# Hybrid encoder step on one core: norm scale of the second layer's first block moved into the first layer's last head, first pair's preparation moved to round 5

## The chip, the cores and the metric

The kernel runs on one NeuronCore of one Trainium2 chip. The metric is the device time of one execution in microseconds (us), and the median of several runs is what counts. The trace names the engines PE (matrix products; PEld are its weight loads), DVE (vector), ACT (scalar), POOL (GpSimd) and SP, whose queue issues all DMAs of this kernel.

## The reference, cut to what matters

One step of a two-layer encoder over 2048 prompt tokens and 8 running streams of 16 tokens, all in float32. Layer 0 is a gated DeltaNet (below: layer A, 8 heads), layer 1 is RWKV-7 (layer B, 16 heads, worked on as 8 pairs).

```python
def rms_norm(x, w):
    return x * rsqrt(mean(x * x, axis=-1) + 1e-6) * w
def trunk(x, ...):
    for i in range(2):
        h = rms_norm(x, norm_w[i])
        y = mixer_a(h, ...) if i % 2 == 0 else mixer_b(h, ...)
        x = x + y
    return rms_norm(x, final_norm_w), ...
def mixer_b(h, x_prev, s0, mu, w_in, ...):
    xx = concat(x_prev, h[:, :-1]) - h
    xs = h + xx * mu[g]                      # g = 0..5
    r, k, v, z = (xs[g] @ w_in[:, g] for g in range(4))
    w_log = -softplus(-(w0 + tanh(xs[4] @ w_w1) @ w_w2)) - 0.5
    a = sigmoid(a0 + (xs[5] @ a_w1) @ a_w2)
    ...                                      # recurrence, group norm, gate with silu(z), @ w_out
```

What the change touches is the factor rsqrt(mean(x * x)) of layer B's norm for the first 256 tokens (the "scale").

## The kernel before, in words

Activations lie with channels on the 128 partitions (8 slices k of the 1024 channels) and tokens along the row. Every large product is made of three float32r matmuls (high part by high, by low, and low weight by high: `gemm`, and L451 to L453, L1059 to L1061), so each weight and each activation is split by an ACT cast and a DVE or POOL subtraction. On first use a weight is loaded raw, split and written back as a pair; later blocks load the pair.

**Layer A** takes five token blocks of 3 or 4 chunks of 128 tokens. `a_steps` counts i over 40 heads of all blocks and three more steps. In step i, `weave` runs side by side: the recurrence of head i-2 (`a_rec`), the Gram matrices and inverse of head i-1 (`a_gram`), the output product of head i-3 (`a_out`), at block ends the next block's norm, and the slots of a stream of large input products. `weave` interleaves generators by the share of the step that each is given; every `yield` ends one slot. At i = 40 the stream of layer A is used up. `swap` (in `layers`) closes the right-hand pool of tiles, opens that of layer B in its place and returns layer B's stream; steps 40, 41 and 42 take 33, 34 and 34 slots of it (AHEAD = 101).

**Layer B** takes six blocks: 128 prompt and 128 sample tokens (NT = 256), then five of 384 tokens. `b_stream` first runs `b_hidden` of block 0: `norm_scale` (8 squares on ACT, 6 additions on DVE and POOL, column sums on PE at L204, rsqrt, spread over the partitions on PE at L216), 18 slots with the 9 idle ones that `wait` = 8 asks for, then the normalised rows H (L991), 4 slots. Then come 136 slots per block of two-product units in the order g = 1 (K), 0 (R), 4 with 5 (the two low-rank products, "LoRA"), 2 (V), 3 (gate z): 8 slots per pair of products, and 6 matmuls in a slot. Their inputs, the lerps x + xx mu, are made by `b_lerp` in up to 8 buffers; most are made in bursts at fixed slots, 16 of them during the LoRA pair. `b_keep` copies a finished product into one of two "kvo" buffers and stores it in DRAM. The LoRA results pass through the same two buffers and are split into the tiles LT, of which there is one copy.

`b_steps` runs 54 steps i of 12 rounds each. In step i: `b_prep` of pair i, `b_subst` of pair i-1, `b_inverse` of i-2, `b_scan` of i-3, `b_gate` of i-4, in odd steps `b_out`, now and then `b_final`, and 17 slots of the stream (PACE; 8 from i = 40 on). `rounds` gives each part the round numbers of its slots; what is left of a part is run in round 12. `b_prep` begins with two products that read LT and the pair's weight w2 (L1120), which `b_load` fetches one step earlier (L1096, split at L1098 and L1099).

PE executes in the order of the program text (MANUAL). For the other engines and the DMA queue a list scheduler sets the order at compile time, by due times that `_due` works out from the next use, and it frees a tile's memory when all its readers are done.

Of the kernel before, what the change touches and what calls it, by code (L numbers as in the profile page):

```python
# [9 lines left out]
F32 = mybir.dt.float32  # L10
# [6 lines left out]
P = 128  # L17
# [54 lines left out]
class _K:  # L72
# [191 lines left out]
    def layers(self):  # L264

        tc, nc = self.tc, self.nc
        ab, bb, off = [], [], 0
        for npc, nsc in A_BLOCKS:
            n = npc + nsc
            ab.append(dict(off=off, npc=npc, nsc=nsc, n=n, NT=n * P, NP=npc * P))  # L270
            off += n * P
        off = 0
        for ncp, nsc in B_BLOCKS:
            nq = ncp + 2 * nsc
            bb.append(dict(off=off, ncp=ncp, nsc=nsc, nq=nq, NP=ncp * 64, NT=nq * 64))
            off += nq * 64
        with ExitStack() as st, ExitStack() as main, ExitStack() as side, tc.manual_schedule(engines=MANUAL):
            self.psum = st.enter_context(tc.tile_pool(name="psum", bufs=1, space=bass.MemoryType.PSUM))
            self.wpool = st.enter_context(tc.tile_pool(name="wpool", bufs=1))
            self.mp = main.enter_context(tc.tile_pool(name="amain", bufs=1))  # L280
            self.sp = side.enter_context(tc.tile_pool(name="aside", bufs=1, side="right"))
            self.a_setup()

            def swap():
                side.close()
                self.sp = side.enter_context(tc.tile_pool(name="bside", bufs=1, side="right", reuse_waits="tile"))
                self.b_setup_side()
                return self.b_stream(bb)
            stream = self.a_steps(ab, swap)
            main.close()  # L290
            self.mp = main.enter_context(tc.tile_pool(name="bmain", bufs=1, reuse_waits="tile"))
            self.b_setup()
            self.b_steps(bb, stream)
# [24 lines left out]
            S.append(s)  # L318
        self.cw, self.hist, self.nw, self.abc, self.nega, self.S = cw, hist, nw, abc, nega, S

    def a_steps(self, blocks, swap):

        nc, n = self.nc, len(blocks) * HA

        def at(i):
            return (blocks[i // HA], i % HA) if 0 <= i < n else None
        st = self.a_stream(blocks, self.a_first(blocks[0]))

        def take(i):
            for end in st:  # L330
                if end and i + 1 < n:
                    return
                yield
        for i in range(n + 3):
            if i == n:
                self.put_conv()
                st = swap()
            parts = []
            if at(i - 2):
                b = at(i - 2)[0]  # L340
                parts.append((self.a_rec(*at(i - 2)), 11 + 3 * b["npc"] + 7 * b["nsc"], 0.3 if i == 2 else 0.0, 1.0))
            if at(i - 1):
                parts.append((self.a_gram(*at(i - 1)), 17, 0.0, 0.95))
            if at(i - 3):
                parts.append((self.a_out(*at(i - 3)), 13, 0.1, 1.0))
            if i % HA == HA - 1 and at(i + 1):
                parts.append((self.a_norm(blocks[i // HA + 1]), 9, 0.0, 0.8))
            if i < n:
                parts.append((take(i), 24 if i % HA else 31, 0.0, 1.0))
            else:  # L350
                m = AHEAD * (i + 1 - n) // 3 - AHEAD * (i - n) // 3
                parts.append((islice(st, m), m, 0.0, 1.0))
            self.weave(parts)
        for h in range(HA):
            nc.sync.dma_start(self.io["o_pd"][h], self.S[h])
        return st
# [571 lines left out]
    def b_steps(self, blocks, st):  # L928

        npair = len(blocks) * KT  # L930
        def at(i):
            return (blocks[i // KT], i % KT) if 0 <= i < npair else None
        self.b_load(*at(0))
        for i in range(npair + 6):
            parts = []
            if at(i):
                parts.append((self.b_prep(*at(i)), range(1, 13)))
            if at(i - 2):
                parts.append((self.b_inverse(*at(i - 2)), (1, 2, 3, 4, 5, 6, 7, 8, 10)))
            if at(i - 4):  # L940
                parts.append((self.b_gate(*at(i - 4)), (1, 2, 3, 6)))
            if at(i - 1):
                parts.append((self.b_subst(*at(i - 1)), range(1, 9)))
            if at(i - 3):
                b = at(i - 3)[0]
                parts.append((self.b_scan(*at(i - 3)), 2 * b["ncp"] + 6 * b["nsc"], 0.0, 1.0))
            j = i - 5
            if at(j) and j % 2 == 0:
                out = self.b_out(blocks[j // KT], (j % KT, j % KT + 1))
                if j < npair - 2:  # L950
                    parts.append((out, 8, 0.5, 1.0))
                else:
                    parts.append((chain(out, self.b_final(blocks[j // KT])), 21, 0.5, 1.0))
            if at(j) and j % KT == KT - 1 and j < npair - 1:
                parts.append((self.b_final(blocks[j // KT]), 13, 0.0, 1.0))
            m = PACE if i < npair - KT else LAST_PACE
            parts.append((islice(st, m), m, 0.0, 1.0))
            self.rounds(ROUNDS, parts)
            if at(i + 1):
                self.b_load(*at(i + 1))  # L960
        for p in range(KT):
            self.nc.sync.dma_start(self.io["o_pw"][p], self.R[p])

    def b_hidden(self, b):

        nc, io = self.nc, self.io
        off, NP, NT, nsc = b["off"], b["NP"], b["NT"], b["nsc"]

        def xs(k):
            x = self.sp.tile([P, NT], F32, name=self.nm("xn"), tag="xn", bufs=2)  # L970
            nc.sync.dma_start(x, self.x1d[:, k, off:off + NT])
            return x
        rb = yield from self.norm_scale(xs, NT, 8 if off == 0 else 0)
        HT = self.sp.tile([P, KT * (1 + NP + (NS * (TS + 1) if nsc else 0))], F32, name=self.nm("H"), tag="H", bufs=1)
        H = HT[:, 0:KT * (1 + NP)].rearrange("p (k t) -> p k t", k=KT)
        nc.gpsimd.tensor_copy(H[:, :, 0:1], self.hc)
        if nsc:
            Hs = HT[:, KT * (1 + NP):].rearrange("p (k s t) -> p k s t", k=KT, t=TS + 1)
            sh0 = self.sp.tile([P, KT, NS], F32, name=self.nm("sh"), tag="sh", bufs=1)
            nc.sync.dma_start(sh0, io["shift_s"])  # L980
            nc.gpsimd.tensor_copy(Hs[:, :, :, 0:1], sh0.unsqueeze(3))

        def cur(k):
            o = [(slice(0, NP), H[:, k, 1:1 + NP], H[:, k, 0:NP], lambda a: a)]
            if nsc:
                o.append((slice(NP, NT), Hs[:, k, :, 1:], Hs[:, k, :, 0:TS], lambda a: a.rearrange("p (s t) -> p s t", t=TS)))
            return o
        for k in range(KT):
            x = xs(k)
            for sl, h, _, v in cur(k):  # L990
                nc.vector.scalar_tensor_tensor(h, v(x[:, sl]), self.nrm[:, 1, k:k + 1], v(rb[:, sl]), op0=MUL, op1=MUL)  # L991
            if k % 2:
                yield
        nc.gpsimd.tensor_copy(self.hc, H[:, :, NP:NP + 1])
        if off + NT == NTOK:
            nc.sync.dma_start(io["o_ph"], self.hc.rearrange("p k o -> p (k o)"))
        if nsc:
            sh = self.sp.tile([P, KT, NS], F32, name=self.nm("sh"), tag="sh", bufs=1)
            nc.gpsimd.tensor_copy(sh.unsqueeze(3), Hs[:, :, :, TS:TS + 1])
            nc.sync.dma_start(io["o_sh"], sh)  # L1000
        b["cur"] = cur
# [667 lines left out]
```

## Time and profile before

| what | us |
|---|---|
| median of 3 runs | 4665.8 |
| lowest and highest | 4654.6 and 4667.97 |
| the profiled execution, own time | 4661.34 |
| its span, first to last instruction | 4659.5 |

The rows below are of the one profiled execution; times in them are us from the start of its span unless marked ns. PEclk is the clock granted to PE as a share of full speed. Number in square brackets: idle time of the engine before the instruction, and who ended it. Layer A ends and layer B begins at about half of the span.

### The profile page before, as it was taken

How to read it: one execution, taken by the hardware profiler on the slowest of the kernel's cores; microseconds unless marked ns; L12 is line 12 of the kernel's file. 1: busy time of each engine (PE TensorE's matmuls, PEld its weight loads, DVE VectorE, ACT ScalarE, POOL GpSimd, SP SyncE). 2: the span in 40 equal slices, each digit the busy share in tenths (PEclk: the TensorE clock that was granted, in tenths of full speed). 3: DMA queues.
4: the chain of work that ended last, by engine and by line, in shares of the span. 5: the costliest groups of instructions: out<-in, count | busy, mean ns of one | idle time of the engine just before them, and what ended most of it. 6: DMA issues, size and time to landing. Idle time of an engine off the chain costs nothing. (4 is left out here: it accounts for less than half of the span.)

```text
span 4659.5 us, 104081 instructions
## 1 busy us (share of the span) xinstructions
PE 4343.3 (93%) x37093; PEld 3733.9 (80%) x37093; DVE 3470.7 (74%) x9203; ACT 2290.0 (49%) x6132; POOL 1735.8 (37%) x2507
## 2 busy tenths in 40 slices
PE   7999999999999999999987889999999999999996
PEld 6788788888888899999986767778787887887775
DVE  6778766686666766767678888877778778777784
ACT  5444544554434444444456655555545446445542
POOL 6555443332111211211103455444434434344441
PEclk8888999999999999999998989999999999999997
DMA  5555665555555666666655666766665665665442
GB/s 189 183 179 177 221 211 177 180 188 157 174 145 146 182 206 185 191 209 185 188 153 173 202 204 215 225 189 188 193 199 162 203 203 165 202 194 148 139 131 70
DMA packets 765670, 842.18 MB, mean 181 GB/s; under 512 B 263480, under 2 KB 497360, under 8 KB 765152
## 3 DMA queue, kind: packets, MB, share of 16 engines
q1 hardware_dynamic: 765152, 835.53, 59.5%
q8 instruction: 294, 4.82, 0.4%
q14 instruction: 224, 1.84, 0.1%
HBM read 632.73 MB, written 202.53 MB: 179 GB/s over the span
## 5 line engine op out<-in xcount | busy, mean ns | idle before, releaser
L451 PE MATMUL ps<-hh,whl 128*128 128x384 f32 (+1 forms) x1960 | 804.7, 411 | 12.4 <-ACT hh L162 10.3
L452 PE MATMUL ps<-hl,whl 128*128 128x384 f32 (+1 forms) x1960 | 718.2, 366 | 2.5 <-DVE hl L163 2.0
L453 PE MATMUL ps<-hh,whl 128*128 128x384 f32 (+1 forms) x1960 | 717.3, 366 | 2.7 <-POOL whl L125 2.7
L1059 PE MATMUL ps<-xh,whl 128*128 128x384 f32 (+1 forms) x1632 | 608.4, 373 | 32.8 <-ACT xh L162 19.0
L1060 PE MATMUL ps<-xl,whl 128*128 128x384 f32 (+1 forms) x1632 | 561.1, 344 | 21.3 <-POOL xl L163 12.4
L1061 PE MATMUL ps<-xh,whl 128*128 128x384 f32 (+1 forms) x1632 | 559.3, 343 | 9.9 <-DVE whl L125 9.6
L125 POOL TENSOR_TENSOR whl<-wraw,whl 128x256 fp32r<-128x256 f32 x454 | 365.9, 811 | 414.4 <-ACT whl L124 389.8
L571 DVE SCALAR_TENSOR_TENSOR cv<-pre,cw,cv 128x512 f32<-128x512 f32 (+3 forms) x576 | 375.3, 659 | 124.8 <-ACT cv L569 117.8
L124 ACT CAST whl<-wraw 128x256 fp32r<-128x256 f32 x726 | 287.8, 402 | 313.2 <-PE ps L453 94.4
L451 PEld LDWEIGHTS ps<-hh,whl 128*128 128x128 f32 x1960 | 377.4, 193 | 69.3 <-issue 18.5
L168 PE MATMUL ps<-oh,whl 128*128 128x384 f32 (+2 forms) x1024 | 392.1, 383 | 27.7 <-DMA whl<-wd 14.9
L453 PEld LDWEIGHTS ps<-hh,whl 128*128 128x128 f32 x1960 | 376.5, 192 | 39.6 <-POOL whl L125 4.2
L452 PEld LDWEIGHTS ps<-hl,whl 128*128 128x128 f32 x1960 | 378.2, 193 | 35.4 <-DVE hl L163 5.8
L1059 PEld LDWEIGHTS ps<-xh,whl 128*128 128x128 f32 x1632 | 322.1, 197 | 76.4 <-ACT xh L162 25.3
L169 PE MATMUL ps<-ol,whl 128*128 128x384 f32 (+2 forms) x1024 | 368.5, 360 | 6.9 <-DVE ol L163 6.7
L170 PE MATMUL ps<-oh,whl 128*128 128x384 f32 (+2 forms) x1024 | 365.3, 357 | 0.7 <-POOL whl L125 0.7
L842 DVE TENSOR_TENSOR sbt<-B,TB 48x15 f32<-48x15 f32 (+14 forms) x1320 | 346.5, 262 | 23.6 <-DMA B<-scr 2.8
L844 DVE TENSOR_TENSOR TB<-TB,sbt 48x15 f32<-48x15 f32 (+14 forms) x1320 | 347.6, 263 | 19.6
L1060 PEld LDWEIGHTS ps<-xl,whl 128*128 128x128 f32 x1632 | 325.1, 199 | 33.1 <-POOL xl L163 16.8
L1061 PEld LDWEIGHTS ps<-xh,whl 128*128 128x128 f32 x1632 | 323.6, 198 | 18.4 <-DVE whl L125 17.8
L820 DVE TENSOR_TENSOR x<-x,ps 128x384 f32<-128x384 f32 (+1 forms) x320 | 191.3, 598 | 91.1 <-PE ps L170 90.7
L168 PEld LDWEIGHTS ps<-oh,whl 128*128 128x128 f32 x1024 | 198.7, 194 | 66.6 <-ACT oh L162 9.6
(349 smaller groups left out, 10268.4 us busy)
## 6 DMA issues: line engine op xcount, KB each, us to landing
whl<-wd SPq DMA_DIRECT2D x1582, 256.0 KB
wd<-whl SPq DMA_DIRECT2D x428, 256.0 KB
wraw<-in_w_a SPq DMA_DIRECT2D x288, 128.0 KB
wraw<-in_w_b SPq DMA_DIRECT2D x256, 128.0 KB
kvd<-kvo SPq DMA_DIRECT2D x160, 192.0 KB
xn<-x1d SPq DMA_DIRECT2D x80, 192.0 KB
wraw<-in_w_ao SPq DMA_DIRECT2D x96, 128.0 KB
xn<-in_x SPq DMA_DIRECT2D x32, 256.0 KB
```

Source lines behind the costliest of these rows:

```text
L125: (self.nc.gpsimd if tag == "o" else self.weng).tensor_tensor(w[:, 1], raw, w[:, 0].bitcast(F32), op=SUB)
L168: self.nc.tensor.matmul(out, lhsT=wh, rhs=hh, start=first and i == 0, stop=False)
L169: self.nc.tensor.matmul(out, lhsT=wh, rhs=hl, start=False, stop=False)
L170: self.nc.tensor.matmul(out, lhsT=wl, rhs=hh, start=False, stop=i == n - 1)
L451: nc.tensor.matmul(p, lhsT=wh[:, k % 2], rhs=hh, start=k == 0, stop=False)
L452: nc.tensor.matmul(p, lhsT=wh[:, k % 2], rhs=hl, start=False, stop=False)
L453: nc.tensor.matmul(p, lhsT=wl[:, k % 2], rhs=hh, start=False, stop=k == KT - 1)
L571: nc.vector.scalar_tensor_tensor(o, f(j), self.cw[:, ct, j:j + 1], o, op0=MUL, op1=ADD)
L844: nc.vector.tensor_tensor(T[:, j + 1:16, 0:j + 1], T[:, j + 1:16, 0:j + 1], o, op=SUB)
L1059: nc.tensor.matmul(o, lhsT=wh[:, i], rhs=xh, start=k == 0, stop=False)
L1060: nc.tensor.matmul(o, lhsT=wh[:, i], rhs=xl, start=False, stop=False)
L1061: nc.tensor.matmul(o, lhsT=wl[:, i], rhs=xh, start=False, stop=k == KT - 1)
```

## The change

While head 39 is the newest of layer A, a new generator `b_ahead` computes the scale of layer B's first block into a tile of layer A's main pool that was used for the first block of layer A; it has 11 shares of the step, between 10% and 90% of it. `b_hidden` of that block then starts with H at once, and loads x into five buffers by turns in place of two. The two slot counts (101 before `b_steps`, then 17 per step) stay, so the stream's products stand 18 slots further on at every later step. In step 0 of `b_steps`, `b_prep` gets the rounds 5 to 12 instead of 1 to 12; its last five pieces then all fall in round 12.

```diff
@@ layers
-            stream = self.a_steps(ab, swap)
+            stream = self.a_steps(ab, bb[0], swap)
@@ a_steps
+            if i == n - 1:
+                ahead = self.b_ahead(after)
...
+            if i == n - 1:
+                parts.append((ahead, 11, 0.1, 0.9))
@@ b_steps
-                parts.append((self.b_prep(*at(i)), range(1, 13)))
+                parts.append((self.b_prep(*at(i)), range(1, 13) if i else (5, 6, 7, 8, 9, 10, 11, 12)))
@@ new
+    def b_ahead(self, b):
+        NT = b["NT"]
+        def xs(k):
+            x = self.sp.tile([P, NT], F32, name=self.nm("xn"), tag="xn", bufs=2)
+            self.nc.sync.dma_start(x, self.x1d[:, k, 0:NT])
+            return x
+        rb = self.mp.tile([P, NT], F32, name=self.nm("rb0"), tag="rb0", bufs=1)
+        b["rb"] = yield from self.norm_scale(xs, NT, 0, rb)
@@ b_hidden
-            x = self.sp.tile([P, NT], F32, name=self.nm("xn"), tag="xn", bufs=2)
+            tag, bufs = ("nacc", self.nacc) if "rb" in b and k % 5 > 1 else ("xn", 2)
+            x = self.sp.tile([P, NT], F32, name=self.nm("xn"), tag=tag, bufs=bufs)
...
-        rb = yield from self.norm_scale(xs, NT, 8 if off == 0 else 0)
+        rb = b["rb"] if "rb" in b else (yield from self.norm_scale(xs, NT))
```

## Rows read from the trace of the kernel before

**Rows 1.** The page, section 1: busy us, share of the span, instructions.
```profile
PE 4343.3 (93%) x37093; PEld 3733.9 (80%) x37093; DVE 3470.7 (74%) x9203; ACT 2290.0 (49%) x6132; POOL 1735.8 (37%) x2507
```

**Rows 2.** Busy time by stretch around the layers' border; columns in the first line.
```profile
core 0: us, PE busy (x) PEld busy (x) DVE busy (x) ACT busy (x) POOL busy (x), PEclk, DMA share, GB/s
2290.00:2335.00 45.00, 44.24 (x293) 42.47 (x293) 33.07 (x92) 19.29 (x51) 8.63 (x18) 1.00 0.64 188
2345.00:2357.00 12.00, 6.58 (x28) 6.03 (x29) 5.88 (x17) 3.32 (x10) 4.32 (x5) 0.57 0.25 66
...
2435.00:2484.00 49.00, 41.22 (x249) 35.32 (x247) 37.72 (x110) 37.66 (x118) 5.52 (x7) 0.93 0.51 162
2492.00:2500.00 8.00, 8.00 (x60) 7.83 (x61) 5.62 (x14) 5.21 (x15) 4.08 (x9) 0.71 0.69 217
```

**Rows 3.** PE's timeline in step 40: start, us, instruction, [idle before <-releaser].
```profile
2336.07 0.83 PE L705 MATMUL ps<-T,L 128*128 128x128 f32 x6
...
2350.84 2.13 PE L204 MATMUL ps<-ones,nacc 128*128 128x1 f32 x8 [4.89 <-DVE nacc L193]
...
2362.49 0.47 PE L1059 MATMUL ps<-xh,whl 128*128 128x256 f32 x1
```

**Rows 4.** Timelines of the DMA queue, ACT and DVE in step 40.
```profile
2337.46 0.85 SPq L971 DMA_DIRECT2D xn<-x1d  x2
...
2339.94 0.87 ACT L188 ACTIVATE nacc<-xn 128x256 f32<-128x256 f32 x2 [1.01 <-DMA xn<-x1d]
...
2357.71 1.14 DVE L991 SCALAR_TENSOR_TENSOR H<-xn,nrm,nrb 128x128 f32<-128x128 f32 x4 [0.38 <-ACT nrb L219]
```

**Rows 5.** Timelines where layer A ends: PE, the DMA queue, ACT.
```profile
2491.72 0.58 PE L1120 MATMUL ps<-LT,w 128*128 128x256 f32 x1 [8.69 <-DVE w L1099]
...
2484.74 0.93 SPq L829 DMA_DIRECT2D x1d<-x  x2
...
2488.04 0.42 SPq L1096 DMA_DIRECT2D w2r<-in_b_w  x1
...
2490.80 0.40 ACT L1098 CAST w<-w2r 128x256 fp32r<-128x256 f32 x1 [4.10 <-DMA w2r<-in_b_w]
```

**Rows 6.** Timelines of PE and DVE: two matmuls and a weight's split.
```profile
2420.69 0.29 PE L1059 MATMUL ps<-xh,whl 128*128 128x256 f32 x1
2420.81 0.28 PE L1060 MATMUL ps<-xl,whl 128*128 128x256 f32 x1
...
2484.35 0.42 DVE L125 TENSOR_TENSOR whl<-wraw,whl 128x256 fp32r<-128x256 f32 x1
```

**Rows 7.** Busy time of steps 1 to 3, 29, 31, 45, 46, 47 of `b_steps` (columns as above).
```profile
2511.30:2617.10 105.80, 85.22 (x705) 70.28 (x704) 92.44 (x286) 62.47 (x176) 49.01 (x83) 0.85 0.54 161
3761.50:3811.50 50.00, 46.56 (x530) 40.45 (x529) 39.54 (x100) 23.94 (x64) 20.28 (x23) 0.97 0.79 234
3849.20:3905.50 56.30, 49.60 (x529) 40.99 (x528) 49.74 (x119) 36.93 (x91) 25.23 (x31) 0.94 0.52 143
...
4445.30:4488.10 42.80, 37.26 (x475) 30.75 (x474) 34.97 (x89) 15.86 (x47) 18.92 (x27) 0.96 0.67 206
4488.10:4516.20 28.10, 26.96 (x428) 22.18 (x427) 24.13 (x73) 15.14 (x46) 14.37 (x17) 1.00 0.35 97
4516.20:4551.60 35.40, 31.59 (x434) 24.86 (x434) 30.02 (x81) 14.80 (x46) 18.29 (x25) 0.90 0.36 89
```

**Rows 8.** Start of step 31 on PE; instructions of LT and L1081 (ns min/median/max).
```profile
3849.17 0.51 PE L1120 MATMUL ps<-LT,w 128*128 128x384 f32 x2
...
3850.71 0.44 PE L1059 MATMUL ps<-xh,whl 128*128 128x384 f32 x1
...
L162 ACT CAST LT<-lt x12: 401/504/515, 2477.6 to 4248.5; 128x384 fp32r<-128x384 f32 x10, 128x256 fp32r<-128x256 f32 x2
L163 DVE TENSOR_TENSOR LT<-lt,LT x12: 417/541/748, 2478.1 to 4257.8; 128x384 fp32r<-128x384 f32 x10, 128x256 fp32r<-128x256 f32 x2
...
L1081 ACT COPY kvo<-ps x144: 347/478/495, 2380.6 to 4381.7; 128x384 f32<-128x384 f32 x120, 128x256 f32<-128x256 f32 x24
```

More of the change, by code (lines that the diff above doesn't have):

```diff
@@ L319, in a_setup, with a_steps @@
         self.cw, self.hist, self.nw, self.abc, self.nega, self.S = cw, hist, nw, abc, nega, S
-    def a_steps(self, blocks, swap):
+    def a_steps(self, blocks, after, swap):
         nc, n = self.nc, len(blocks) * HA
```

## The prediction

> **What bounds the kernel now.** I read the page first: PE is busy 93% of the span, DVE 74% [rows 1]. So time is PE's work plus PE's idle time plus what it loses at the half clock, and a change that only moves work can win nothing but idle and half-clock time. Next the busy time by stretch around the border of the layers [rows 2]: during head 39 (2290 to 2335) PE is busy 44.24 of 45 us at full clock while DVE has 11.9 us to spare, ACT 25.7 and POOL 36.4. Right behind it, from 2345 to 2357, PE is busy 6.58 of 12 us and the granted clock is 0.57 on average, that is mostly at the lower of its two levels, 1.2 of 2.4 GHz. PE's timeline names the cause [rows 3]: it waited 4.89 us until 2350.84 for the norm's sums, at L204, and layer B's first product comes only at 2362.49. The second hole is where layer A ends [rows 5]: 8.69 us before L1120, which waits for the split weight w2; its load was issued at 2488.04, behind the last stores of layer A (2484.74), and its cast ran at 2490.80. After that hole the clock was 0.71 for 8 us [rows 2]. These two holes are what the change aims at.
>
> **The change part by part.** First the moved scale. Eight squares on ACT, six additions (three on DVE, three on POOL), two small sets of matmuls and eight loads of x on SP's queue now run beside head 39. They fit in the spare time of every engine there [rows 2], and SP spends 0.43 us on one issue (0.85 for two [rows 4]), 3.4 us in 45; I cost this at nothing. What hides it is head 39's PE work: were PE to wait there for the sums too, it would cost about the 4.89 us that it costs now. Taken out of step 40: 4.89 us of idle, and 6.58 us of work at 0.57, which at full clock is 3.8, so 2.8 more; together **-8**, rounded.
>
> What is late next in step 40: `b_hidden` now starts at once, so the first product stands in slot 5 of 33 instead of 23, and PE, which keeps program order, gets there after a few matmuls of head 38 (L705, about 2336.9 [rows 3]). Its input needs x, H, a lerp and its split. x was issued at 2337.46 and there at 2339.94; from H's first write (2357.71 [rows 4]) to the first product (2362.49 [rows 3]) it took 4.8 us with other DVE work between. Kept as they are, these give 2339.9 + 4.8 - 2336.9 = 7.8 us of idle. Head 39 no longer blocks x with the norm's buffers and x gets five buffers, so it may come some 3 us earlier; then 5. Behind that the first eight lerps meet head 38's own DVE work. I take **+6**, ends +2 and +14 (7.8, doubled for the lerps behind it).
>
> The stream stands 18 slots further on. Six 256-wide matmuls, 0.12 us apart [rows 6], make 0.72 us a slot: 13 us of PE work go into steps 40 to 42. At the end the same 18 slots are missing from steps 44 to 47, at 384 columns: step 45 with eight slots takes 42.8 us, step 47 with one takes 35.4 [rows 7], so a slot is worth 1.06 us there, 19 in all. The difference, 6 us, is paid between, where 18 slots become 384 wide. PE's sum is zero; what counts is idle time:
> - *The end.* Step 47 shows that an odd step without the stream is shorter by the stream's full share. Step 46 has DVE busy 24.13 of 28.1 us [rows 7], so of its 8.5 us only about 4 can go. **+5** of idle, ends 0 and +10 (both 45 and 46 bound by DVE).
> - *Steps 1 to 3 and step 42.* Steps 1 to 3 take 105.8 us with DVE busy 87% and PE 85.22 us at a clock of 0.85 [rows 7]; 18 weight splits of 0.42 us on DVE [rows 6], 7.6 us, leave them. In step 42 (about 2435 to 2484) PE is idle 7.8 us at a clock of 0.93 [rows 2]; six of its lerps move to step 41, where I count them as hidden by PE. Not all of the relief turns into time, since PE gets 6 us more there: **-8**, ends 0 and -14.
> - *The burst of 16 lerps* makes step 31 last 56.3 us, against 50.0 for step 29, an odd one without it [rows 7]. One step further on it falls into an even step. I see no reason for either sign: 0, ends -5 and +5 over all blocks.
>
> The first pair's preparation in round 5: five stream slots now stand ahead of L1120, 3.6 us at the pace of [rows 6], a little more with waits, and they also keep PE going. The load of w2 still follows layer A's stores, so of the 8.69 us about 4 stay, and of the half clock (8 us at 0.71, 2.3 us lost [rows 2]) perhaps nothing. **-7**, ends -11 (all of it) and 0 (the slots lack inputs, or the five pieces that fall in round 12 make PE wait instead).
>
> **A new wait.** LT has one copy. In the kernel before, the next block's LoRA pair ended in step 8k+7, after that step's L1120 had read LT; 18 slots further on it ends in step 8k+6, at slot 9, while pair 8k+7 reads the old LT in rounds 1 and 2 of the next step. Until then the LoRA results hold both kvo buffers, the next pair's products (V) can't be copied out, and PE's slot in round 1 waits for their PSUM bank. From L1120 on, three operations follow each other: LT's cast 0.50, its subtraction 0.54, V's copy 0.48 [rows 8], 1.5 us behind the end of L1120; today the stream's product comes 1.54 us after L1120's start, of which L1120 takes 0.51 [rows 8]. So at least 0.5 us is missing, twice (two banks), in each of the steps 7, 15, 23, 31 and 39; busy queues add to it. I take 1.2 us a block, **+6**, ends 0 (later idle time absorbs it) and +15 (3 us a block). The second copy of kvd is reused earlier too; its store has to follow the last load of z, some three rounds earlier, so I put it at 0; if not, SP waits as long as for w2 (2.8 us [rows 5]) in four blocks, +11.
>
> **The sum:** -8 + 6 + 5 - 8 + 0 - 7 + 6 = -6 us. From the profiled execution's 4661.34 that is 4655.3; this execution lies 4.5 us under the median, and from the median, which is what is measured, it is **4659.8 us**.
>
> **The rivals.**
> - *The waits don't bite* (first product 2 us late, LT's wait absorbed, the end fully won): -8 + 2 + 0 - 8 - 11 + 0 = -25, 4640.8 us. For it: step 47's length, and PE's gaps that a later surplus can fill. Against it: DVE's 86% in step 46.
> - *LT's casts block ACT (slower).* If the cast of LT is queued on ACT ahead of its turn, it stands from the LoRA pair's end (round 7) to L1120 of the next step with everything behind it. In [rows 5] ACT stood idle 4.10 us before a cast that waited for its load while PE starved. The rival decides from 2.4 us a block on (12 us eat the other terms' gain) and gives over 0.3% from 5.2; at 8 us a block it is -12 + 40 = +28, 4693.8 us. Against it: a scheduler that places the cast when LT is free. The Trainium skill (PSUM — Partial Sum Buffer, "Engine vs sequencer instructions") says that the queues of ScalarE, VectorE and GpSimdE are strictly first in, first out. The trace agrees as far as the 4.10 us go; by that rule every ACT operation behind the cast would wait with it, which is this rival.
> - *The hole only moves* (first product at the late end, nothing else changed): -6 + 8 = +2, 4667.8 us. For it: the norm's wait and the first lerps' wait are both about 5 to 8 us.
>
> **How the numbers follow.** About 0.3%, 14 us, is what a measurement of this kernel tells from no change. Forecast 0.47 (own range -16 to +6), first rival 0.29, LT rival 0.12, moved hole 0.12. Faster: the first rival and a tenth of the forecast, 0.34. Slower: the LT rival and a little of the moved hole, 0.13. The same: 0.53. The range reaches below the first rival and, for the kvd and LT terms, above the median: 4639 to 4678; it leaves out most of the LT rival and the tail below.
>
> **What would show it.** Right: no L204 wait in step 40 and the first L1059 before 2348; L1120's first wait at 3 to 5 us; in step 7 and the like a short PE wait in round 1 or 2 ended by ACT L1081; the stream ending in step 44, with step 46 at 23 to 25 us. Wrong: a wait of over 10 us early in step 40, ACT idle before LT's cast, or steps 45 and 46 as long as before.

## The result, and the profile after it

The changed kernel took 4693.6 us (median of 6 runs, 4686.7 to 4709.8) against 4662.5 before: ratio 1.0079, 95% interval 1.0057 to 1.0102. It is slower by 0.8%, 31 us; measured once more, beside the last experiments, it was 1.0098 (1.0073 to 1.0122). The forecast was 4659.8, the range ended at 4678. The profiled execution took 4689.5 us, its span is 4687.7. In the changed kernel the line numbers of layer A are 4 higher, those of layer B 16 (L1120 is L1136, L1059 is L1075).

PE does the same work [rows 1]. The page's first section after:

```profile
PE 4331.4 (92%) x37093; PEld 3727.0 (80%) x37093; DVE 3509.8 (75%) x9203; ACT 2290.2 (49%) x6132; POOL 1740.2 (37%) x2507
```

So the loss has to be idle time of PE, or time at the lower clock. To find its place I cut both traces at the same events. The cut begins at one product of layer A that waits 0.95 us in both (L744 before, L748 after; 1951.46 and 1953.07 us). Then come the start of step 0 of `b_steps`, step 8, step 40, step 44 and the end. First the view of busy time by stretch for the kernel before:

```profile
core 0: us, PE busy (x) PEld busy (x) DVE busy (x) ACT busy (x) POOL busy (x), PEclk, DMA share, GB/s
1951.46:2491.72 540.26, 502.21 (x3382) 475.00 (x3382) 383.16 (x1103) 261.84 (x728) 93.63 (x183) 0.98 0.62 184
2491.72:2796.13 304.41, 260.68 (x2235) 212.27 (x2235) 260.90 (x806) 181.10 (x506) 157.75 (x242) 0.89 0.62 196
2796.13:4267.75 1471.62, 1371.49 (x15947) 1167.18 (x15947) 1163.06 (x3043) 783.74 (x2112) 659.66 (x808) 0.96 0.65 192
4267.75:4412.86 145.11, 134.29 (x1801) 112.19 (x1801) 112.60 (x318) 70.32 (x205) 64.80 (x84) 0.91 0.49 136
4412.86:4659.52 246.66, 198.32 (x2683) 161.58 (x2682) 169.03 (x464) 97.25 (x297) 87.72 (x106) 0.87 0.36 105
```

The same view of the changed kernel:

```profile
1953.07:2506.88 553.81, 518.08 (x3520) 493.50 (x3520) 395.37 (x1134) 274.34 (x765) 94.06 (x183) 0.97 0.61 184
2506.88:2818.69 311.81, 258.35 (x2205) 211.60 (x2205) 262.87 (x803) 177.06 (x496) 149.45 (x242) 0.89 0.66 208
2818.69:4295.49 1476.80, 1365.49 (x15947) 1162.78 (x15947) 1190.83 (x3018) 778.41 (x2094) 669.98 (x807) 0.96 0.65 190
4295.49:4437.01 141.52, 130.64 (x1801) 109.58 (x1801) 115.19 (x323) 70.48 (x205) 65.68 (x84) 0.93 0.52 141
4437.01:4687.75 250.74, 184.42 (x2575) 148.28 (x2574) 165.15 (x458) 95.13 (x291) 85.55 (x106) 0.80 0.29 80
```

Length less PE's busy time is idle time. Up to step 0: 38.1 before, 35.7 after. Steps 0 to 7: 43.7 and 53.5. Steps 8 to 39: 100.1 and 111.3. Steps 40 to 43: 10.8 and 10.9. From step 44 on: 48.3 and 66.3. Together 241.1 and 277.7, **36.6 us more idle time**, and of the relief at the border that the forecast counted on 2.4 us. PE's busy time is 10.0 us less in the changed kernel, so the five stretches are 26.6 us longer. The instruction counts show the moved work: 138 more matmuls stand ahead of step 0 (108 are the 18 slots; 30 are the five slots that round 5 puts ahead of the first L1136, where I let step 0 begin), 30 fewer in steps 0 to 7, 108 fewer behind step 44. Step 0 starts 13.6 us later for it, but the end, 18 slots poorer, is 4.1 us *longer*.

**At the border** the two holes that the change aimed at [rows 3, 5] did change. PE's timeline after:

```profile
2340.31 0.83 PE L709 MATMUL ps<-T,L 128*128 128x128 f32 x6
...
2349.64 0.58 PE L1075 MATMUL ps<-xh,whl 128*128 128x256 f32 x1 [8.50 <-ACT xh L162]
...
2506.88 0.50 PE L1136 MATMUL ps<-LT,w 128*128 128x256 f32 x2 [1.89 <-DVE w L1115]
```

The wait for the norm's sums is gone, and it doesn't turn up in head 39: PE is idle for 0.28 us from 2253.07 to 2336.07. The wait for w2 is 1.89 us, not 8.69. But the first product of layer B now waits 8.50 us. What it waited for stands in the timelines of the DMA queue, DVE and ACT:

```profile
2341.18 2.33 SPq L987 DMA_DIRECT2D xn<-x1d  x5
2343.56 0.43 SPq L908 DMA_DIRECT2D mu<-in_b_mu  x1
...
2343.49 3.13 DVE L1007 SCALAR_TENSOR_TENSOR H<-xn,nrm,rb 128x128 f32<-128x128 f32 x10 [1.44 <-POOL H L997]
2346.55 0.17 DVE L909 TENSOR_SCALAR mu<-mu 128x48 f32<-128x48 f32 x1
...
2346.82 1.28 ACT L1024 ACTIVATE xt<-H,mu 128x128 f32<-128x128 f32 x4 [4.84 <-DVE mu L909]
```

The last thing missing for a lerp is its factor mu. Its load went out at 2343.56, behind five loads of x, and L909, which makes it ready on DVE, ran behind ten operations of H with no idle time of DVE before it; which of the two made it late isn't told apart. I had x, H and the lerp in the sum, and not mu.

**At the end**, the rows are step 44, step 45, step 46 and the rest, first before (its steps 45 and 46 are in [rows 7]), then after:

```profile
4412.86:4445.30 32.44, 30.69 (x446) 25.72 (x446) 29.32 (x81) 18.61 (x54) 18.99 (x20) 0.95 0.49 144
...
4516.20:4659.52 143.32, 103.41 (x1339) 82.92 (x1338) 80.60 (x223) 47.64 (x150) 35.43 (x44) 0.80 0.24 68
```

```profile
4437.01:4467.90 30.89, 29.56 (x439) 24.43 (x438) 26.74 (x76) 18.17 (x54) 15.40 (x18) 0.94 0.32 92
4467.90:4512.70 44.80, 30.94 (x432) 24.71 (x428) 34.47 (x91) 15.10 (x46) 21.53 (x28) 0.85 0.53 145
4512.70:4536.00 23.30, 20.36 (x380) 15.89 (x378) 21.14 (x64) 14.46 (x44) 11.16 (x12) 0.85 0.18 47
4536.00:4687.75 151.75, 103.56 (x1333) 83.25 (x1332) 82.80 (x231) 47.40 (x148) 37.46 (x48) 0.76 0.23 63
```

Step 45 has no slot of the stream any more and takes 44.8 us, where with eight it took 42.8. Step 46 falls from 28.1 to 23.3, and what follows takes 8.4 us more. The granted clock of 45 and 46 is 0.85, where it was 0.96 and 1.00. PE's waits in these steps, two of before and then three of after:

```profile
4447.74 0.92 PE L1281 MATMUL ps<-T,N 64*64 64x64 f32 x24 [1.95 <-POOL T L1265]
...
4458.05 0.69 PE L1185 MATMUL ps<-ones,ch 64*64 64x1 f32 x18 [0.60 <-POOL ch L1158]
```

```profile
4473.30 1.54 PE L1297 MATMUL ps<-T,N 64*64 64x64 f32 x24 [4.74 <-POOL T L1281]
...
4485.86 1.12 PE L1201 MATMUL ps<-ones,ch 64*64 64x1 f32 x18 [4.97 <-POOL ch L1174]
...
4545.48 1.55 PE L1297 MATMUL ps<-T,N 64*64 64x64 f32 x24 [8.89 <-POOL T L1281]
```

At the third place the kernel before has no wait. So these three waits are 18.6 us where they were 2.6: 16 of the 18.0 us that the end has more. T is the end of a chain that runs over three steps: the pair's preparation, its store and reload, 30 small serial operations of DVE (`subst`), another store and load, then POOL. My reading is that with no stream beside it PE gets ahead of that chain and waits for it.

**In the stream**, the waits for LT's copies are there, twice in each of the steps 7, 15, 23, 31 and 39. PE and ACT in step 31 [rows 8 shows it before]:

```profile
3881.69 0.52 PE L1136 MATMUL ps<-LT,w 128*128 128x384 f32 x2
...
3884.93 0.44 PE L1075 MATMUL ps<-xh,whl 128*128 128x384 f32 x1 [1.10 <-ACT kvo L1097]
...
3888.74 0.45 PE L1075 MATMUL ps<-xh,whl 128*128 128x384 f32 x1 [0.97 <-ACT kvo L1097]
```

```profile
3883.03 0.49 ACT L162 CAST LT<-lt 128x384 fp32r<-128x384 f32 x1
3883.55 0.58 ACT L1140 ACTIVATE ch<-ps,hp 128x384 f32<-128x384 f32 x1
3884.03 0.47 ACT L1301 COPY Z<-ps 128x384 f32<-128x384 f32 x1
3884.40 0.48 ACT L1097 COPY kvo<-ps 128x384 f32<-128x384 f32 x1
```

L1097 stands behind LT's cast, as foreseen, and behind two operations of other parts (behind one to four in the other places). The Trainium skill (PSUM — Partial Sum Buffer, "Engine vs sequencer instructions") has ACT's queue strictly first in, first out; the four rows, each starting when the one ahead is about done, agree. The two waits are 2.1 to 2.8 us a block, 11.2 us in all five. In step 7 ACT stood idle right ahead of both casts, until L1136 had read LT:

```profile
2775.14 0.51 ACT L162 CAST LT<-lt 128x384 fp32r<-128x384 f32 x1 [1.75 <-PE ps L1136]
...
2778.52 0.51 ACT L162 CAST LT<-lt 128x384 fp32r<-128x384 f32 x1 [0.60 <-PE ps L1136]
```

DVE shows a second difference in steps 8 to 39: it is busy for 1190.8 us with 3018 operations, where it was 1163.1 with 3043. The other profiles with a lead of 101 and 17 slots in these steps have 1191 to 1195 us, those with 83 and 17 slots 1167 to 1169. Why fewer operations keep it busy longer I didn't trace, nor what that costs.

### The profile page after: what moved, and what is told of

It reads as the page before. It is cut to its first block, busy times and chain, and to the rows that moved or that the text cites. A ratio compares the mean times of both kernels' runs of the same rounds, so it can differ in the third digit from the quotient of the medians.

```text
span 4687.7 us, 104130 instructions
## 1 busy us (share of the span) xinstructions
PE 4331.4 (92%) x37093; PEld 3727.0 (80%) x37093; DVE 3509.8 (75%) x9203; ACT 2290.2 (49%) x6132; POOL 1740.2 (37%) x2507
## 3 DMA queue, kind: packets, MB, share of 16 engines
q1 hardware_dynamic: 765152, 835.53, 59.5%
## 4 chain that ended last, share of the span: by engine, by line
PE 56%; DVE 24%; DMA 7%; ACT 5%; issue 4%; POOL 3%; SPq 1%; POOLq 0%; DVEq 0%; ACTq 0%
PE ps L455 6%; PE ps L456 6%; PE ps L457 6%; PE ps L168 4%; PE ps L169 4%; PE ps L170 4%; DVE sbt L846 4%; PE ps L1075 4%; DVE TB L848 3%; PE ps L1076 3%; PE ps L1077 3%; DMA wraw<-in_w_b 2%; DVE cv L575 1%; DMA whl<-wd 1%; PE ps L1224 1%
## 5 line engine op out<-in xcount | busy, mean ns | idle before, releaser
L1075 PE MATMUL ps<-xh,whl 128*128 128x384 f32 (+1 forms) x1632 | 604.5, 370 | 57.4 <-ACT xh L162 25.2
L1076 PE MATMUL ps<-xl,whl 128*128 128x384 f32 (+1 forms) x1632 | 559.3, 343 | 18.4 <-POOL xl L163 11.2
L455 PEld LDWEIGHTS ps<-hh,whl 128*128 128x128 f32 x1960 | 376.5, 192 | 70.2 <-issue 18.6
L168 PE MATMUL ps<-oh,whl 128*128 128x384 f32 (+2 forms) x1024 | 385.7, 377 | 23.9 <-DMA whl<-wd 11.7
L1075 PEld LDWEIGHTS ps<-xh,whl 128*128 128x128 f32 x1632 | 322.2, 197 | 99.4 <-ACT xh L162 29.5
L846 DVE TENSOR_TENSOR sbt<-B,TB 48x15 f32<-48x15 f32 (+14 forms) x1320 | 367.5, 278 | 27.7 <-DMA B<-scr 3.5
L170 PE MATMUL ps<-oh,whl 128*128 128x384 f32 (+2 forms) x1024 | 359.9, 351 | 0.0
L1077 PEld LDWEIGHTS ps<-xh,whl 128*128 128x128 f32 x1632 | 324.6, 199 | 11.2 <-DVE whl L125 10.9
```

What stands on the lines that cost most here:

```text
L168: self.nc.tensor.matmul(out, lhsT=wh, rhs=hh, start=first and i == 0, stop=False)
L170: self.nc.tensor.matmul(out, lhsT=wl, rhs=hh, start=False, stop=i == n - 1)
L455: nc.tensor.matmul(p, lhsT=wh[:, k % 2], rhs=hh, start=k == 0, stop=False)
L846: nc.vector.tensor_tensor(o, B[:, j + 1:16, j:j + 1].to_broadcast([rows, m, j + 1]), T[:, j:j + 1, 0:j + 1].to_broadcast([rows, m, j + 1]) ...
L1075: nc.tensor.matmul(o, lhsT=wh[:, i], rhs=xh, start=k == 0, stop=False)
L1076: nc.tensor.matmul(o, lhsT=wh[:, i], rhs=xl, start=False, stop=False)
```

## The experiments

After the profile there were three theories. **END**: the 18 slots that leave the last steps win nothing there. **LT**: the copy waits and what follows from them. **BORDER**: the changed order at the border itself loses the time. The lead, the number of slots taken ahead of `b_steps`, is one constant: with 83 in place of 101 the products stand where they stood before, since the 18 slots of the scale are gone. Each ratio is to the kernel before, measured beside the run.

**Lead of before.** First kernel: all of the change but its longer lead.

```diff
-AHEAD, PACE, LAST_PACE, ROUNDS = 101, 17, 8, 12
+AHEAD, PACE, LAST_PACE, ROUNDS = 83, 17, 8, 12
```

> The change with 83 instead of 101 slots of the stream before the pair steps, so that every later step finds the stream where it stood before the change (LT read before it is overwritten, stream ending in step 47). Theory END (the 18 slots taken out of steps 44 to 47 shorten nothing there, because the chain of one pair's steps bounds them: about 19 us): 4655 to 4667 us, no slower than before. Theory LT (waits for the single copy of LT, 8 us a block): the same, 4650 to 4665. Theory BORDER (the holes only moved, and the late preparation makes a new one in step 2): 4672 to 4685, since these stay.

Measured: 4661.75 us, ratio 1.0003 (0.9991 to 1.0015). The whole loss goes with the lead; the changed order costs nothing by itself, which is against BORDER. It wins nothing either.

**Half of it**, a lead of 91 (the same constant).

> The change with 91 slots: the stream is 8 slots further on than before, so that LT is again read before it is overwritten, while 8 slots are missing at the end. END: the run with 83 slots plus 0.45 of the loss, 6 to 9 us above it. LT: within 3 us of the run with 83. BORDER: within 3 us of the run with 83, both near 4680.

Measured: 4671.86, ratio 1.0022 (1.0008 to 1.0036). From step 0 on this has no copy waits at L1097, and 8 of the 18 slots are missing. By the ratios it is 9 us above the lead of 83, which is END's figure and not that of the other two, but the two intervals overlap.

**The last slots spread**: with the longer lead, five slots a step at the end in place of eight (LAST_PACE = 5), so that the missing ones are spread over the last steps.

> The change with 5 instead of 8 slots a step from step 40 on, so that the 39 slots left there last to step 47 as before; the stream's lead and the five LT waits stay. END: 8 to 16 us below the changed kernel, 4678 to 4686. LT: as the changed kernel, 4689 to 4697. BORDER: as the changed kernel, 4689 to 4697.

Measured: 4699.59, ratio 1.0087 (1.0068 to 1.0106). Wrong for END in its simple form, and above the other two as well. 12 slots more stand behind step 44 than in the changed kernel, and idle time there falls to 59.5 us, but steps 40 to 43 have 23.0 us where they had 10.9. In this run too the missing slots left a hole where they were missing.

**Without round 5**: the first pair's preparation starts in round 1 as before, all else as changed.

```diff
-                parts.append((self.b_prep(*at(i)), range(1, 13) if i else (5, 6, 7, 8, 9, 10, 11, 12)))
+                parts.append((self.b_prep(*at(i)), range(1, 13)))
```

> The change without its second part: the first pair's preparation in rounds 1 to 12. BORDER: the 11.6 us wait of step 2 goes and the w2 wait before L1120 comes back as 8 to 9 us: 4685 to 4693, 0 to 8 below the changed kernel. END and LT: 4693 to 4700, the seam's wait comes on top.

Measured: 4697.81, ratio 1.0078 (1.0059 to 1.0098). The round makes no difference that can be told. PE waits 13.00 us for T in step 2 here, so that wait doesn't come from round 5, as BORDER had it, and 6.88 us for w2.

**The early scale alone**: the lead of 83 and no round 5.

> The early scale alone: the lead as before (83 products, so the copy waits of LT and the 18 missing slots of the end are gone) and the first pair's preparation from round 1 as before. It differs from the kernel with the lead of 83 (4661.8 us, ratio 1.000) by round 5 alone. If the gain at the border (5.4 us at the start of step 0) is given back in steps 2 and 3 because round 5 sets the preparation late, this one keeps it: 4654 to 4658. If it is given back because the chain preparation, substitution, inverse has its own length whatever starts it (the view that the first version of this chain, with round 5 taken out of the changed kernel, supports: 4697.8 against 4693.6), no difference: 4659 to 4666, a ratio within 0.2% of 1.

Measured: 4650.56 beside 4656.15 for before, ratio 0.9994 (0.9979 to 1.0010). No difference to before, nor to the run with round 5 (1.0003), as the second view had it. Its first product waits 8.81 us, and the wait for w2 is back at 8.88.

**The lead shortened by two slots**, 99 in place of 101.

> The lead shortened by two slots only (99 instead of 101, 16 slots more than before). The product that waits for a new copy of LT then falls at a step's border, so the short waits of PE at each block's first product should mostly go. If the loss of the change is the 16 to 18 slots that leave the end (END), it stays: 4690 to 4693, 2 us less than the changed kernel. If the waits for LT were most of it (LT), it falls by their cost, 6 to 11 us: 4681 to 4686 for one block's worth of waits in each of the five blocks seen.

Measured: 4664.72, ratio 1.0020 (1.0006 to 1.0034). Two slots of 1.06 us took back three quarters of the loss, more than either theory said. PE's waits on L1097 from step 4 to 39 are 14.6 us in the changed kernel and 0.1 here. A second wait went with them: PE waited 9.7 us for POOL's L1350, mostly in the steps 18, 26 and 34, and waits 0.7 here. With the longer lead of two slots the LoRA pair's end falls on the wrong side of the step's border. What makes L1350 late once in eight steps I didn't trace. Not all waits fall: in steps 8 to 39 PE waits 29.4 us for DVE's L1408 in the changed kernel and 44.3 here. So the run shows what two slots are worth together, and not what LT's waits are worth by themselves.

**Slots given back**: the changed kernel, with its 18 slots taken out of steps 32 to 39, so that the end is as before.

```diff
-            m = PACE if i < npair - KT else LAST_PACE
+            m = (PACE if i < npair - 2 * KT else 15 if i < npair - KT - 2 else 14) if i < npair - KT else LAST_PACE
```

> The changed kernel with the 18 slots of its longer lead given back in the last block before the end: steps 32 to 37 take 15 slots for 17, steps 38 and 39 take 14, so that steps 40 to 47 have the slots of before. Steps 32 to 39 lose 18 slots of 1.06 us, and the end is as before. END (steps 44 to 47 have a length of their own, whatever slots they have): 14 to 19 us less than the changed kernel, 4675 to 4680. If steps 32 to 39 are bound by the same chain as the end, so that slots taken out of them win nothing either: 4690 to 4695. The copy waits of LT stay in the first four blocks in either case.

Measured: 4670.64, ratio 1.0032 (1.0018 to 1.0045), 22 us under the changed kernel's first ratio (0.47% of 4660). Behind step 44 this kernel is idle for 45.8 us, before 48.3, the changed one 66.3. Taken out of steps 32 to 39 the slots do win their time; out of the end they don't.

**The mirror**: the lead of 83, so no copy waits, and 18 slots more in steps 32 to 39 (19 in six of them, 20 in two), so that the end misses them.

> The mirror of the run that gives the slots back: the lead is as before (83 products), and 18 slots are put into steps 32 to 39 (19 in six of them, 20 in two) instead of at the border, so steps 44 to 47 have the slots that they have in the changed kernel, with no long lead and with no waits for LT in the first four blocks. END: the time of the kernel with the lead of 83 (4661.8) and 14 to 19 us more, 4676 to 4681. If the end is not bound by itself and the lead's loss lies elsewhere (LT, the border): within 5 us of that kernel, 4657 to 4667.

Measured: 4680.11, ratio 1.0051 (1.0031 to 1.0070). That is 22 us over the lead of 83 by the ratios (18 by the medians), as END said: the 18 slots cost their time in steps 32 to 39, and the end, without them, wins none back, with 65.3 us idle behind step 44 for 47.9.

**The changed kernel again**, beside the next three.

> The changed kernel once more, beside the three below on one chip. Its first ratio was 1.0079 from 6 runs; the profiles, counted from a fixed product of layer A at about 1944 us, say 26.6 us more than before for it, 15.0 with 18 slots given back, 15.3 for a lead of 99 (measured 15 and 9 us). If the profiles tell it right, 4680 to 4692 (ratio 1.005 to 1.008). If the first measurement was high by chance, below 4678.

Measured: 4706.92, ratio 1.0098, above both expectations; its interval (1.0073 to 1.0122) overlaps with that of the first ratio.

**Another queue.** In the changed kernel's profile PE waited 11.55 us in step 2 for the first pair's T. The store sc2b stood on SP behind two stores of the next pair. SP's stores, the end of sc2b's data on DVE (L851), and PE's wait:

```profile
2565.40 1.25 SPq L1249 DMA_DIRECT2D scrb<-N  x2
2566.74 0.55 SPq L1261 DMA_DIRECT2D sc2b<-TB  x1
```

```profile
2560.16 0.36 DVE L851 COPY TB<-TB 32x256 f32<-32x256 f32 x1
```

```profile
2571.97 0.69 PE L1297 MATMUL ps<-T,N 64*64 64x64 f32 x8 [11.55 <-POOL T L1281]
```

The scheduler puts the stores in that order with a lead of 101 or 99 (without round 5 between the two); before and with 83 the sc2b store stands first. (The text below says that the order differs at 99; it is the same, but N came early there.) So it went by ACT's queue:

```diff
+        eng = nc.scalar if (b["off"], q) == (0, 0) else nc.sync
-        nc.sync.dma_start(sc2.rearrange("t (b x) -> b t x", x=256), TB[0:nb].rearrange("p t r c -> p t (r c)"))
+        eng.dma_start(sc2.rearrange("t (b x) -> b t x", x=256), TB[0:nb].rearrange("p t r c -> p t (r c)"))
...
-            nc.sync.dma_start(cm, sc2[t].rearrange("(c p k) -> p c k", p=P, k=16))
+            eng.dma_start(cm, sc2[t].rearrange("(c p k) -> p c k", p=P, k=16))
```

> In the changed kernel the store of the first pair's inverted blocks (sc2b) stands on SP's queue behind the two stores of the second pair's N: its data are ready at 2559.9, it is issued at 2566.1, 6.2 us later, and PE waits 11.55 us for what follows. With a lead of 99, whose order differs, the store goes out 0 us after its data and that wait is 6.25. Here that one store and its two loads go by ACT's queue instead. Theory QUEUE: the wait in step 2 falls to 5 or 6 us and steps 0 to 3 shorten by 5 to 8 us, so 5 to 8 us less than the changed kernel. Rival (the chain of the first pair is late for other reasons, and PE finds its next wait at once): within 3 us of it.

Measured: 4693.38, ratio 1.0068 (1.0046 to 1.0091), and the wait in step 2 of this run, then of the changed kernel's second profile:

```profile
2560.37 0.69 PE L1298 MATMUL ps<-T,N 64*64 64x64 f32 x8 [7.97 <-POOL T L1282]
```

```profile
2572.76 0.69 PE L1297 MATMUL ps<-T,N 64*64 64x64 f32 x8 [5.15 <-POOL T L1281]
```

That is inconclusive: the median is 13.5 us under that of the changed kernel beside it, but the intervals overlap. The second profile of the changed kernel has the same order on SP, its data came later (2566.7), the store had no delay, and the wait was 5.15 without any help. Over all 14 profiles the late store and the long wait go together: where the store went out 5.2 to 6.2 us behind its data (changed, last slots spread, no round 5, 18 given back) that wait is 10.6 to 13.0 us, and where it went out at once 0.5 to 8.0. With a lead of 101 or 99 the first four have 48.6 to 53.5 us of idle time in steps 0 to 7, the other four 44.0 to 46.4. Whether that lasts to the end of the kernel isn't shown.

**Idle slots at the border**: the early scale alone, with six empty slots between the first lerps and the first product.

```diff
+        for _ in range(6):
+            yield
         for b, units in pairs:
...
-AHEAD, PACE, LAST_PACE, ROUNDS = 83, 17, 8, 12
+AHEAD, PACE, LAST_PACE, ROUNDS = 89, 17, 8, 12
```

> The early scale alone (as the run of that name: lead of before, first preparation from round 1), with six empty slots between the first lerps and the first product, so that PE has the products of layer A's last heads while ACT and DVE make the lerps. If the 8.8 us wait of the first product is what took the place of the wait for the norm's sums: that wait falls below 3 us, step 0 starts 4 to 8 us earlier against layer A's fixed product (541 for 547), and the time is 3 to 8 us under the run without empty slots (4645 to 4652 where before is 4656). If the border has a length of its own (the other engines' work): the wait turns up elsewhere before step 0, and the time is within 3 us of that run.

Measured: 4656.77 beside 4660.6, ratio 0.9992 (0.9976 to 1.0008). The first product's wait:

```profile
2345.29 0.58 PE L1077 MATMUL ps<-xh,whl 128*128 128x256 f32 x1 [2.56 <-ACT xh L162]
```

It fell from 8.81 to 2.56, and step 0 starts 535.7 us behind the common product where it was 540.3 in the run without empty slots: as expected. But the idle time up to step 0 is 37.1 us for 36.0, so other waits took the place of the shortened one (4.1 us at L728 for T, 1.9 for ACT's L1093); what is shorter is PE's busy time, 498.6 us for 504.3, at a granted clock of 0.98 for 0.96. Steps 0 to 7 then take 307.8 us against 303.3, and the total is the same. By idle time the second view holds, that the wait turns up elsewhere; from one profile of each, it isn't shown that a gain at the border was there and was given back.

**The lead of 99 with its 16 slots given back** (15 slots in each of the steps 32 to 39).

> The lead of 99 with its 16 slots given back in steps 32 to 39 (15 slots each for 17), so that steps 40 to 47 are as before. The 18 slots given back in the changed kernel were worth 22 us by the medians and 12 us by the profiles' totals. END: 10 to 18 us under the lead of 99 (ratio 1.002), that is 0.998 to 1.000 of before. If with 16 slots the end was not lengthened (its tail took 395.1 us against 391.7 before): within 5 us of the lead of 99, ratio 1.001 to 1.003.

Measured: 4657.37, ratio 0.9989 (0.9971 to 1.0008), 14 us under the lead of 99 by the ratios: END again, with 16 slots. It is level with before and the lowest ratio of all; none of the kernels can be told to beat before.

PE's idle time from the common product on, by stretch, from the same view of each run's one profile:

| kernel | to step 0 | 0 to 7 | 8 to 39 | 40 to 43 | from 44 | sum | ratio |
|---|---|---|---|---|---|---|---|
| before | 38.1 | 43.7 | 100.1 | 10.8 | 48.3 | 241.1 | 1 |
| changed | 35.7 | 53.5 | 111.3 | 10.9 | 66.3 | 277.7 | 1.0079 |
| changed, again | 36.9 | 46.4 | 111.6 | 10.9 | 65.3 | 271.2 | 1.0098 |
| no round 5 | 42.1 | 53.4 | 115.7 | 11.7 | 66.4 | 289.4 | 1.0078 |
| last slots spread | 36.3 | 51.9 | 114.2 | 23.0 | 59.5 | 284.9 | 1.0087 |
| other queue | 34.1 | 45.7 | 114.2 | 13.5 | 64.6 | 272.0 | 1.0068 |
| 18 given back | 36.9 | 48.6 | 106.8 | 11.7 | 45.8 | 249.8 | 1.0032 |
| lead 99 | 36.2 | 44.0 | 97.4 | 12.6 | 63.4 | 253.6 | 1.0020 |
| lead 99, 16 given back | 37.4 | 44.7 | 100.5 | 12.4 | 48.8 | 243.8 | 0.9989 |
| lead 91 | 36.8 | 53.5 | 106.2 | 8.5 | 57.2 | 262.1 | 1.0022 |
| lead 83 | 33.8 | 55.8 | 107.9 | 10.8 | 47.9 | 256.2 | 1.0003 |
| lead 83, 18 from the end | 33.5 | 54.0 | 101.6 | 8.9 | 65.3 | 263.4 | 1.0051 |
| early scale alone | 36.0 | 44.1 | 100.8 | 11.4 | 49.7 | 242.0 | 0.9994 |
| the same, idle slots | 37.1 | 50.2 | 102.1 | 11.8 | 49.0 | 250.2 | 0.9992 |

The column from step 44 on is the clearest: 63 to 66 us wherever 16 or 18 slots are missing in those steps, 57 with 8, 60 with 6 (the last slots spread, where 12 more are missing just ahead), and 46 to 50 where none is. In steps 8 to 39 a lead of 101 has 107 to 116, the others 97 to 108; the two overlap (the lead of 83 has 107.9 without a copy wait, and level with before all the same), so the part of LT rests on its waits and on the pairs of runs that differ by two slots. The column ahead of step 0 holds nothing for any theory. Nor does the sum alone rank the kernels: 18 given back has 249.8 us at 1.0032, the lead of 83 has 256.2 at 1.0003.

## Why the prediction was wrong, point by point

The sum was -6 us, the measured difference +31 (first) and about +46 (again). By its own terms:

- **Step 40, -8 for the norm's wait and +6 for the first product**: the wait went (right), the first product waited 8.50 us for a forecast of 6, inside the ends 2 to 14. Two parts were off: x was issued 0.9 us after the start of head 38's products (L709) where it was 1.4 before (L705), and not 3 us earlier; and from H's first write to the first product it took 6.15 us for 4.8, since the term lacked mu, which came last. First product at 2349.64 and not before 2348, by the clock of the span; counted from the common product it came 14.5 us earlier than before (411.0 and 396.6 us behind it).
- **The seam, -7**: the wait fell from 8.69 to 1.89 (the text said 3 to 5), the term's size is right. But idle time ahead of step 0 is only 2.4 us less in all; other waits for lerps and for layer A's last products grew beside it. The step that failed is that these terms were added, as if a hole that is filled stayed filled. The rival "the hole only moves" describes the border rightly, and its sum, 4667.8, fails on the other terms.
- **Steps 1 to 3 and 42, -8**: the relief of DVE came (92.4 us busy in steps 1 to 3 before, 85.6 and 83.9 after), and those steps got 0.8 us shorter in the first profile and 5.6 in the second. But step 0, for which the sum had no term, got 8.7 and 9.8 us longer, at a granted clock of 0.64 and 0.66 for 0.87, since the stream's work of step 1 now stands there. Steps 0 to 7 have 9.8 and 2.7 us more idle time. In step 2 PE waits 11.55 and 5.15 us for T; that this chain sets the pace there is my reading. Step 42 can't be told apart. Step 0 before (steps 1 to 3 are in [rows 7]), then steps 0 and 1 to 3 after (first profile):

```profile
2491.72:2511.30 19.58, 18.59 (x140) 17.24 (x141) 13.94 (x34) 9.84 (x28) 7.72 (x14) 0.87 0.71 222
```

```profile
2506.88:2535.12 28.24, 23.53 (x128) 21.10 (x129) 21.07 (x50) 14.29 (x41) 13.70 (x21) 0.64 0.55 175
2535.12:2640.07 104.95, 82.18 (x688) 70.11 (x687) 85.59 (x267) 55.81 (x152) 47.84 (x77) 0.84 0.65 200
```

- **The end, +5 of idle time, 14 of 19 us won back**: measured +18.0 of idle time and a stretch that is 4.1 to 7.8 us longer. By idle time this is the largest miss. It failed at "step 47 shows that an odd step without the stream is shorter by the stream's full share". I read it so: step 47 was short because step 46, still filled by eight slots, had given the chain time; with 45 and 46 empty PE catches up with T and `ch` and waits 4.74, 4.97 and 8.89 us. That these three waits are where the time went is read from the timeline; that the end wins nothing is shown by three pairs of runs (the changed kernel with 18 given back, the lead of 99 with 16 given back, the lead of 83 with 18 taken). The stream did end in step 44 and step 46 did take 23.3, as said, so the two signs were right and the reading that they mean a gain was not; "steps 45 and 46 as long as before" came true for 45. The granted clock adds to it: from step 44 on it was 0.87 before, 0.80 after, so that 108 matmuls fewer saved 13.9 us of PE's busy time (9.1 in the second profile, at 0.79) and not the 19 of the slots at the step's pace.
- **LT, +6**: right in mechanism, place and sign, but 11.2 us in size (2.1 to 2.8 us a block for 1.2): ACT had one to four other operations between LT's cast and the copy. Waits for L1350, 9.7 us, come and go with the same two slots of lead, and the sum had no term for them. By the ratios the two slots are worth 27 us or more, of which the idle time of the profiles shows 18 to 24. By time this is a miss about as large as that of the end, and only its first 11.2 us have a named cause.
- **The burst, 0**: the 16 lerps now fall in the even steps (step 6 takes 55.7 us, before 35.8, step 7 43.9 for 63.1), no measurable sum. **kvd, 0**: no such wait was seen.

The LT rival's number, 4693.8, is the measured one, but not for its reason, and that is chance. Its sign, ACT idle ahead of LT's cast, was there in step 7 (1.75 and 0.60 us); in the steps 15 to 39 ACT stood idle for 3.9 us one operation further ahead, before L1485, which waited for DVE's L1473 and does so in other steps and in the kernel before too. No block's waits for the copy came to more than 2.8 us, where the rival had 8. The chance of 0.12 stood on a cost that wasn't there, and the 0.34 for faster on a rival that took the end as fully won.

Added up from the profile: -2.4 (border), +9.8 (first steps, 2.7 in the second profile), +11.2 (stream), +18.0 (end) make the 36.6 us of idle time. That the stream's 11.2 equals the 11.2 us of waits for LT's copies is chance: 2.8 of those lie in step 7, and steps 8 to 39 have other waits that came and went. That the lead makes the whole loss, that the end wins nothing and that the last two slots of the lead cost some 27 us by themselves are shown by runs; how those two slots cost more than the waits for LT is open. That the first steps lose for good is not shown, since the two profiles differ there by 7 us from each other. A second copy of LT, which would have taken its waits away by themselves, wasn't run; nor was an earlier load of mu.

## What to carry to other kernels

Work that fills holes is worth something only where it is missed less than where it is put: before you move it ahead, look at the place it leaves, above all at a tail that a chain bounds, since that tail keeps its length and loses its cover. A removed wait at a border is a gain only if no other wait grows in its place; here waits of 4.89 and 8.69 us went or shrank, and the idle time ahead of step 0 fell by 2.4 us. And a shift of a long stream has a phase: of 101 and 99 slots ahead, one had a buffer's reuse on the wrong side of a step in all five blocks, so try the neighbours of such a constant.

## What was not expected of the hardware

The same instructions don't take PE the same time in each execution. Steps 8 to 39 have 15,947 recorded matmuls in both the kernel before and the early scale alone; PE was busy with them for 1371.5 us at a granted clock of 0.96 and 1358.3 us at 0.97, with 100 us idle in both. The two profiles of the changed kernel itself have 1365.5 and 1370.7 us there. A single profile's lengths can't tell 13 us in that stretch, while idle times agreed within 1 us (in steps 0 to 7 those of the changed kernel's two profiles differ by 7); this is why the table above compares idle time, and the ratios of several runs decide.
